# Feed forward of a hybrid decoder layer: right factors built in small steps, factor tiles regrouped, three units on unnormalised input, another order of plain and seven-product units

## The chip, the cores and the metric

One core of a Trainium2 chip. The metric is the device time of one execution in microseconds. Engines are named as the profile does: PE is TensorE's matrix product and PEld its weight load, DVE is VectorE, ACT is ScalarE, POOL is GpSimd, SP is SyncE, which issues nearly all DMAs.

## The reference, cut to what matters

One inference step of one decoder layer: 512 prompt tokens and 8 sample tokens (520 columns here), model width 1024. A mixer (retention, dilated attention, gates) is followed by a feed forward; the change touches the feed forward alone.

```python
h = h + mix
h = h + swiglu(rmsnorm(h, ln2_g), w_ffn_in, w_ffn_out)
y = rmsnorm(h, lnf_g)

def swiglu(xn, w_ffn_in, w_ffn_out):
    a, b = jnp.split(xn @ w_ffn_in, 2, axis=-1)     # hidden width 2816 = 22 x 128
    return (jax.nn.silu(a) * b) @ w_ffn_out
```

Everything is float32. To come near to that on TensorE, every operand of a product is split in two float32r parts: a high part (a copy, rounded) and a low part (operand minus high part). A product is then three: high x high, high x low, low x high.

## The kernel before, in words

**Layout.** Activations lie transposed: 128 rows of the model width per tile, 520 columns in two halves of 260 (HF). Weights stream from HBM as 194 pieces of 128 x 1024 (`raw`, four buffers, each loaded by SP when the low part of an earlier piece is done). Each piece falls into blocks of 128 x 512. For each block ScalarE makes the high part (`wh`, line 200) and VectorE the low part (`wl`, line 203), with six buffers of each; `advance` (lines 213 to 221) keeps them five blocks ahead of TensorE.

**The feed forward's order.** Hidden unit i (0 to 21) stands for 128 rows of a and 128 rows of b. `FFSEQ` (lines 28 to 32) lists the work: "in" 0 to 8, four "out" steps for the hidden rows 0 to 7, "in" 9 to 16, four "out" steps for rows 8 to 15, "in" 17 to 21. After the loop `LAST` and what follows it do the output for rows 16 to 21.

**Plain units.** `ffn_in(i)` calls `unit` twice, once for a and once for b: 8 steps of 6 products of 260 columns, 96 products per hidden unit, into a pair of PSUM banks. There are two such pairs, used in turn, so the evacuation of one half frees the bank pair that the half after the next writes. Silu(a) is made by ScalarE, the multiplication by b (`middle`) by VectorE.

**Seven-product units (quads).** The units in `INQ` and all eight "out" steps in the loop run through `quad` (line 285) instead, by Strassen's scheme in Winograd's form: seven products of half-size factors in the place of eight, 84 matrix products. `SEVEN` (line 283) lists for each of the seven products j the bank (0, 1 or 2) and the right factor x: bank 0 serves j = 0, 2, 4 and 6, bank 1 serves j = 1 and 5, bank 2 serves j = 3. Bank 0 (and 1) goes on accumulating after ScalarE has copied an intermediate state into a snapshot (`s`, line 312, after j = 0, 1, 2, 4). So the product j = 2 waits for the snapshot of j = 0, j = 4 for that of j = 2, j = 6 for that of j = 4. The next quad's first product writes what was bank 1, which the addition at line 1323 reads after j = 5; its second product writes what was bank 0, which the multiplication at line 1331 reads after j = 6. VectorE also makes the sums of weight blocks (lines 184, 188, 190).

**Right factors.** A quad needs, for each pair k of 128-row blocks, the four parts (two blocks, two halves) and four differences of them (one of the eight is unused on the output side), each as a high and a low part.
- For the input, `gen_factors` (line 1221) makes the normalised input, first the parts (lines 1227 to 1231), then the differences (lines 1242 to 1254), into `XH` and `XL`. It is a generator that advances by one step at each `pump`.
- For the output, `right` (line 315) works on `UF`, which holds the four parts of a pair of hidden units: four operations of 260 columns on VectorE, a copy of 1820 columns on ScalarE (line 321) and a subtraction of 1820 columns on VectorE (line 322). It is called after each odd unit up to 15, at one go; only the subtraction is deferred by three pumps.

**What sets the order.** Each engine works through its instructions in the order in which the program issues them. `pump` (line 123) is called between groups of products, 16 times in a plain unit and 14 times in a quad. It issues the operations that `later` has deferred and then advances the tracks named in `pattern` by one step each; P is the track in use in the feed forward. `finish` advances a track until a given generator is done.

**The unnormalised units.** The norm's factor `rs2` is known only after the last block of h. Units 0 and 1 (`NX = 2`, line 1265) therefore run on `X2`, the input without that factor, and multiply the result by `rs2` at evacuation (lines 1293 and 1302), one more VectorE operation for each half. From unit 2 the products read `XH` and `XL`. `UH`, the right factors' high parts, takes the place of `X2` after unit 1 (line 1364).

Of the kernel before, what the change touches and what calls it, by code (L numbers as in the profile page):

```python
# [18 lines left out]
HF, HT = 260, 256  # L19
# [18 lines left out]
def tile_hybrid_layer(  # L38
# [9 lines left out]
    V, A, G_, PE, SP = nc.vector, nc.scalar, nc.gpsimd, nc.tensor, nc.sync  # L48
# [3 lines left out]
    bpool = ctx.enter_context(tc.tile_pool(name="bpool", bufs=1))  # L52
# [9 lines left out]
    def halves(ap):  # L62
        return ap.rearrange("p (f c) -> p f c", f=2)
# [10 lines left out]
    def f32(ap):  # L74
        return ap.bitcast(F32)
# [24 lines left out]
    pattern = ["P"]  # L100
# [3 lines left out]
    def later(n, fn):  # L104
        delayed.append([n, fn])
# [176 lines left out]

    SEVEN = ((0, 0), (1, 3), (0, 4), (2, 1), (0, 5), (1, 2), (0, 6))

    def quad(xh, xl, snap, evac):

        s = pos[0] // 8
        pos[0] += 16
        nkp = QUADS[s]

        turn["busy"] ^= 1
        pms = {}
        for _ in range(2):
            i = turn["next"]
            pms[i] = bank_pair(i)[:, 0, :HF]
        out = [pms[turn["busy"]], pms[1 - turn["busy"]], None]
        begun = set()
        for j, (bank, x) in enumerate(SEVEN):
            advance(bid[s, 0] + j)
            if bank == 2:  # L300
                out[2] = abank("pc")[:, :HF]
            h, l = split[bid[s, 0] + j]
            for k in range(nkp):
                ks = slice(k * 128, k * 128 + 128)
                for w, r in ((h, xh), (h, xl), (l, xh)):
                    PE.matmul(out[bank], w[:, ks], r[:, k, x, :], start=bank not in begun, stop=k == nkp - 1 and r is xh and w is l,  # L306
                              skip_group_check=True)
                    begun.add(bank)
                if k % 2:
                    pump()  # L310
            if j in (0, 1, 2, 4):
                A.activation(snap[(0, 3, 1, None, 2)[j]], out[bank], AF.Copy)  # L312
            evac(j, out[bank])

    def right(t, hi, lo):

        V.tensor_tensor(t[:, 3, :], t[:, 0, :], t[:, 7, :], op=ALU.subtract)
        V.scalar_tensor_tensor(t[:, 4, :], t[:, 2, :], -1.0, t[:, 3, :], op0=ALU.mult, op1=ALU.subtract)
        V.tensor_tensor(t[:, 5, :], t[:, 2, :], t[:, 7, :], op=ALU.subtract)
        V.scalar_tensor_tensor(t[:, 6, :], t[:, 4, :], -1.0, t[:, 1, :], op0=ALU.mult, op1=ALU.subtract)  # L320
        A.activation(hi, t[:, 0:7, :], AF.Copy)
        later(3, lambda: V.tensor_tensor(lo, t[:, 0:7, :], f32(hi), op=ALU.subtract))
# [891 lines left out]


    pattern[:] = ["P"]
    XH = bpool.tile([128, 32, HF], F32R, tag="bg", name="XH")
    XL = fp.tile([128, 32, HF], F32R, name="XL")
    XH4, XL4 = (u.rearrange("p (k x) c -> p k x c", x=8) for u in (XH, XL))

    def gen_factors():
        yield from gen_norm2()
        xs = {}

        def one(c, out):
            x = ftmp("xn")
            V.scalar_tensor_tensor(x, hT[:, c, :], g2v[:, c:c + 1], rs2, op0=ALU.mult, op1=ALU.mult)
            xs[c] = x
            hi, lo = (u[:, c // 2, 1:3, :] if c % 2 else u[:, c // 2, 0::7, :] for u in (XH4, XL4))
            A.activation(hi, halves(x), AF.Copy)  # L1230
            later(2, lambda: V.tensor_tensor(lo, halves(x), f32(hi), op=ALU.subtract))

        for c in range(8):
            one(c, None)
            yield
            yield
        for k in range(4):
            x1, x2 = xs.get(2 * k), xs.get(2 * k + 1)
            if k < 3:
                x1, x2 = ftmp("xn"), ftmp("xn")  # L1240
                for c, x in ((2 * k, x1), (2 * k + 1, x2)):
                    V.scalar_tensor_tensor(x, hT[:, c, :], g2v[:, c:c + 1], rs2, op0=ALU.mult, op1=ALU.mult)
# [44 lines left out]
    def ffn_in(i):  # L1287
        s = {}

        def ev_fa(pm, s=s):  # L1290
            t = ftmp("fa")
            if i < NX:
                V.tensor_tensor(halves(t), pm, halves(rs2), op=ALU.mult)
                A.activation(t, t, AF.Silu)
            else:
                A.activation(halves(t), pm, AF.Silu)  # L1296
            s["a"] = t

        def ev_fb(pm, i=i, s=s):
            if i < NX:  # L1300
                t = ftmp("fb")
                V.tensor_tensor(halves(t), pm, halves(rs2), op=ALU.mult)
                pm = halves(t)
            middle(i, lambda out: V.tensor_tensor(out, pm, halves(s["a"]), op=ALU.mult))

        src = (lambda k: (X2[:, k, :], X2[:, 8 + k, :])) if i < NX else xnsrc
        pa = unit(8, src, ev_fa if i else None)
        pb = unit(8, src, ev_fb if i else None)
        if i == 0:
            while not normed:  # L1310
                run_delayed()
                step("P")
            ev_fa(pa)
            ev_fb(pb)

    def ffn_in_quad(i):
        s12, s35 = snaps()
        t = ftmp("fa")

        def evac(j, bank):  # L1320
            if j in (3, 5):
                f = (j - 3) // 2
                V.tensor_tensor(t[:, f * HF:(f + 1) * HF], bank, s12[:, f, :], op=ALU.add)
                if f:
                    A.activation(t, t, AF.Silu)
            elif j == 4:
                later(1, lambda: V.tensor_tensor(s35[:, 0, :], s35[:, 0, :], s35[:, 1, :], op=ALU.add))
            elif j == 6:
                def mult(out):
                    for f, x in ((1, s35[:, 0, :]), (0, bank)):  # L1330
                        V.scalar_tensor_tensor(out[:, f, :], x, -1.0, t[:, f * HF:(f + 1) * HF], op0=ALU.mult, op1=ALU.mult)  # L1331
# [254 lines left out]
```

## Time and profile before

| | |
|---|---|
| median of 3 runs | 1333.28 us (1331.69 to 1336.47) |
| profiled execution | 1334.04 us, its span 1332.2 us |
| mean granted TensorE clock | 0.989 |
| PE busy | 1285.9 us (97%) |
| DVE busy | 818.0 us (61%) |
| ACT busy | 570.6 us (43%) |
| feed forward "in" units 0 to 4 | about 928 to 1003.9 us |
| from unit 5 to unit 21 with the eight "out" steps | 1003.9 to 1280.6 us |

How to read the rows. A row of a group names line, engine, operation, output and inputs, shapes and count, then busy time, mean nanoseconds of one, idle time of the engine before them and what ended it. A row of an engine's timeline has start, duration, engine, line, operation and, in brackets, the idle time before it and its releaser. A row of the chain of waits has start, duration, engine, output and line; "x36" counts instructions. A row of the windows has the stretch, its length, the busy time of PE, PEld, DVE, ACT and POOL with counts, the granted clock, the DMA share and GB/s. TensorE's products are pipelined: 260 columns start every 0.12 us though each is shown with 0.28.

### The profile page before, as it was taken

To read this page: it belongs to the slowest core of one execution; us is meant where nothing else is said; L and a number is where in the kernel's file an instruction comes from. 1 tells how busy PE (TensorE), PEld (TensorE's weight loads), DVE (VectorE), ACT (ScalarE), POOL (GpSimd) and SP (SyncE) were. 2 spreads that over 40 slices of the span, in tenths; PEclk is the share of its full clock that TensorE was granted. 3 is DMA by queue.
4 is the path that set the end of the run, shared out by engine and by line. 5 is a ranking of instruction groups with operands and counts; after the bars stand their busy time and mean duration, and the time that the engine had idled before them with its cause. 6 is when DMAs were issued, how large, how long until landed. Compare 5 with 4: busy or idle time off the path is not lost.

```text
span 1332.2 us, 25611 instructions
## 1 busy us (share of the span) xinstructions
PE 1285.9 (97%) x10465; PEld 1251.6 (94%) x10465; DVE 818.0 (61%) x1713; ACT 570.6 (43%) x1080; POOL 83.3 (6%) x69
## 2 busy tenths in 40 slices
PE   8999999999999999999999999999879999999997
PEld 7999999998988999999999999999879899999997
DVE  7867636747655523244545455486777787679765
ACT  4564334535453522243444433333344455445542
POOL 3601001010002000000000000030000000000000
PEclk9999999999999999999999999999989999999999
DMA  6266236646484232454645556433223232233321
GB/s 219 81 229 229 90 117 206 225 143 230 145 301 157 84 99 89 135 148 127 185 135 171 161 159 205 160 118 122 63 64 96 74 114 84 80 98 112 101 87 65
DMA packets 89783, 183.35 MB, mean 138 GB/s; under 512 B 12025, under 2 KB 33945, under 8 KB 89665
## 3 DMA queue, kind: packets, MB, share of 16 engines
q1 hardware_dynamic: 88944, 180.64, 43.0%
q8 instruction: 82, 1.34, 0.4%
q10 hardware_dynamic: 720, 1.07, 0.2%
q14 instruction: 37, 0.30, 0.1%
HBM read 155.70 MB, written 25.98 MB: 136 GB/s over the span
## 4 chain that ended last, share of the span: by engine, by line
PE 84%; DVE 7%; DMA 3%; issue 3%; ACT 2%; POOL 1%; SPq 1%; DVEq 0%; ACTq 0%
PE pm L250 58%; PE pm L306 11%; PE sp L331 3%; PE pc L306 2%; DMA vb<-vd 2%; PE sp L560 2%; PE sp L578 2%; DVE wl L203 1%; PE pm L1474 1%; PE sp L970 1%; PE sp L512 1%; ACT wh L200 1%; PE sp L920 1%; PE oacc L673 1%; PE sacc L1115 1%
## 5 line engine op out<-in xcount | busy, mean ns | idle before, releaser
L250 PE MATMUL pm<-X,wh 128*128 128x260 f32 x3328 | 550.7, 287 | 4.7 <-DVE X L363 3.6
L250 PEld LDWEIGHTS pm<-X,wh 128*128 128x128 f32 x3328 | 460.5, 189 | 19.4 <-issue 8.3
L203 DVE TENSOR_TENSOR wl<-raw,wh 128x512 fp32r<-128x512 f32 x384 | 275.0, 720 | 165.6 <-ACT wh L200 162.0
L250 PE MATMUL pm<-X,wl 128*128 128x260 f32 x1664 | 336.2, 284 | 0.0
L200 ACT ACTIVATE wh<-raw 128x512 fp32r<-128x512 f32 x384 | 238.7, 625 | 210.1 <-PE pm L250 159.1
L250 PEld LDWEIGHTS pm<-X,wl 128*128 128x128 f32 x1664 | 257.8, 189 | 0.4 <-DVE wl L373 0.4
L306 PE MATMUL pm<-XH,wh 128*128 128x260 f32 x288 | 83.2, 289 | 11.6 <-ACT s L312 9.4
L250 PE MATMUL pm<-GA,wh 128*128 128x260 f32 x512 | 82.2, 283 | 0.0
L306 PE MATMUL pm<-XL,wh 128*128 128x260 f32 x288 | 81.8, 284 | 0.0
L306 PE MATMUL pm<-XH,wl 128*128 128x260 f32 x288 | 81.6, 283 | 0.0
L250 PEld LDWEIGHTS pm<-GA,wh 128*128 128x128 f32 x512 | 70.1, 188 | 0.0
L306 PEld LDWEIGHTS pm<-XH,wh 128*128 128x128 f32 x288 | 54.5, 189 | 14.1 <-ACT s L312 10.6
L250 PE MATMUL pm<-XH,wh 128*128 128x260 f32 x256 | 53.2, 290 | 9.9 <-ACT fa L1296 5.4
L628 ACT ACTIVATE kv<-vb,ks 128x512 f32<-128x512 f32 x64 | 44.2, 714 | 29.6 <-DMA vb<-vd 29.0
L340 POOL TENSOR_TENSOR r<-v,cst 128x4 f32<-128x4 f32 (+4 forms) x14 | 17.6, 1261 | 609.1 <-DVE v L338 609.1
L306 PE MATMUL pm<-UH,wh 128*128 128x260 f32 x192 | 54.4, 283 | 0.9 <-DVE UF L1331 0.9
L306 PEld LDWEIGHTS pm<-XL,wh 128*128 128x128 f32 x288 | 54.7, 190 | 0.0
L306 PEld LDWEIGHTS pm<-XH,wl 128*128 128x128 f32 x288 | 54.6, 190 | 0.0
L306 PE MATMUL pm<-UL,wh 128*128 128x260 f32 x192 | 54.2, 282 | 0.0
L203 DVE TENSOR_TENSOR wl<-qq,wh 128x512 fp32r<-128x512 f32 x60 | 41.2, 687 | 21.1 <-ACT wh L200 20.8
L306 PE MATMUL pm<-UH,wl 128*128 128x260 f32 x192 | 54.1, 282 | 0.0
L663 DVE SCALAR_TENSOR_TENSOR st<-st,kv 128x512 f32<-128x512 f32 x64 | 45.3, 712 | 12.5 <-ACT kv L628 12.5
(324 smaller groups left out, 2185.7 us busy)
## 6 DMA issues: line engine op xcount, KB each, us to landing
raw<-wall SPq DMA_DIRECT2D x192, 512.0 KB
st<-state SPq DMA_DIRECT2D x64, 256.0 KB
out<-st SPq DMA_DIRECT2D x64, 256.0 KB
area<-ck SPq DMA_DIRECT2D x24, 512.0 KB
vb<-vd SPq DMA_DIRECT2D x32, 256.0 KB
area<-qd SPq DMA_DIRECT2D x12, 512.0 KB
cb<-cd SPq DMA_DIRECT2D x4, 768.0 KB
xr<-xT SPq DMA_DIRECT2D x8, 260.0 KB
```

Source lines behind the costliest of these rows:

```text
L200: A.activation(h, r, AF.Copy)
L203: V.tensor_tensor(l, r, f32(h), op=ALU.subtract)
L250: PE.matmul(pm[:, f, :HF], w, x[f] if isinstance(x, tuple) else x[:, f * HF:(f + 1) * HF], start=first, stop=last)
L306: PE.matmul(out[bank], w[:, ks], r[:, k, x, :], start=bank not in begun, stop=k == nkp - 1 and r is xh and w is l, skip_group_check=True)
L331: PE.transpose(out, in_, ident[:n, :n])
L340: G_.tensor_tensor(r[:rows, :ncol], v[:rows, :ncol], mhalf[:rows].to_broadcast([rows, ncol]), op=ALU.pow)
L512: PE.matmul(sp[:, :T - i0], x[:, dt, jb * 128:(jb + 1) * 128], y[:, dt, i0:], start=i == 0, stop=i == len(mm) - 1)
L560: PE.matmul(sp[:, i0:], v[x][:, jb, c * 128:(c + 1) * 128], scs[y][:, SCO[jb]:SCO[jb] + T - i0], start=jb == 0 and x == y, stop=jb == 3 an ...
L578: PE.matmul(sp, kt[x][:, jb, dt * 128:(dt + 1) * 128], v[y][:, jb, :], start=jb == 0 and x == y, stop=jb == 3 and x == 1)
L628: A.activation(kvs[i][:, :DV], vbs[b], AF.Copy, scale=ks[:, dt, b:b + 1])
L663: V.scalar_tensor_tensor(sts[i], sts[i], GAMMA[h], kvs.pop(i)[:, :DV], op0=ALU.mult, op1=ALU.add)
L673: PE.matmul(acc[32 * j:32 * j + 32, :], om[:, bb, :], ys[bb], start=b == 3, stop=b == NS - 1, tile_position=(0, 32 * j), skip_group_check= ...
```

## The change

- `INQ` names other units: plain are now 0 to 5, 8, 12, 16 and 20 (before: 0 to 4, 7, 10, 13, 16 and 19). Both lists have 12 quads.
- `NX` is 3: unit 2 also runs on the unnormalised input.
- `right` becomes a generator on track S with 12 steps; its copy and its subtraction are cut into pieces of 780, 520 and 520 columns. It is pushed after the odd units from 3 on; for the pair (0, 1) it is pushed in the evacuation of unit 2 and finished there at once, ahead of unit 2's own multiplication, which overwrites `UF`. Each even unit and each first "out" step finishes what is left.
- The pattern is "PS" instead of "P".
- The input's factors lie in `XP` (high and low of the parts) and `XT` (high and low of the differences) instead of `XH` (high of all eight) and `XL` (low of all). The differences are split in two halves of 520 columns each, with one step between copy and subtraction.
- In a quad's last evacuation the multiplication that reads the bank comes before the one that reads the snapshot.
- `UH` is opened in the evacuation of unit 2, ahead of `right`.

```diff
-INQ = (5, 6, 8, 9, 11, 12, 14, 15, 17, 18, 20, 21)
+INQ = (6, 7, 9, 10, 11, 13, 14, 15, 17, 18, 19, 21)
...
-    def quad(xh, xl, snap, evac):
+    def quad(factor, snap, evac):
...
-                for w, r in ((h, xh), (h, xl), (l, xh)):
-                    PE.matmul(out[bank], w[:, ks], r[:, k, x, :], start=bank not in begun, stop=k == nkp - 1 and r is xh and w is l,
+                for w, i in ((h, 0), (h, 1), (l, 0)):
+                    PE.matmul(out[bank], w[:, ks], factor(i, k, x), start=bank not in begun, stop=k == nkp - 1 and w is l,
                               skip_group_check=True)
...
-    XH = bpool.tile([128, 32, HF], F32R, tag="bg", name="XH")
-    XL = fp.tile([128, 32, HF], F32R, name="XL")
+    XP = bpool.tile([128, 2, 4, 4, HF], F32R, tag="bg", name="XP")
+    XT = fp.tile([128, 2, 4, 4, HF], F32R, name="XT")
...
-            hi, lo = XH4[:, k, 3:7, :], XL4[:, k, 3:7, :]
-            A.activation(hi, t, AF.Copy)
-            yield
-            yield
-            V.tensor_tensor(lo, t, f32(hi), op=ALU.subtract)
-            yield
+            for j in (0, 2):
+                hi, lo = XT[:, 0, k, j:j + 2, :], XT[:, 1, k, j:j + 2, :]
+                A.activation(hi, t[:, j:j + 2, :], AF.Copy)
+                yield
+                V.tensor_tensor(lo, t[:, j:j + 2, :], f32(hi), op=ALU.subtract)
+                yield
...
+    pattern[:] = ["PS"]
     push("P", gen_factors())
...
-    NX = 2
+    NX = 3
...
+        if i == NX - 1:
+            rights.append(push("S", right(UF, 0)))
+        if i % 2 == 0 and rights:
+            finish("S", rights[-1])
         mult(UF[:, 1:3, :] if i % 2 else UF[:, 0::7, :])
         if i % 2 and i > 1:
-            k = i % 8 // 2
-            right(UF, UH4[:, k], UL4[:, k])
+            rights.append(push("S", right(UF, i % 8 // 2)))
...
+    def right(t, k):
+
+        yield
+        V.tensor_tensor(t[:, 3, :], t[:, 0, :], t[:, 7, :], op=ALU.subtract)
+        V.scalar_tensor_tensor(t[:, 4, :], t[:, 2, :], -1.0, t[:, 3, :], op0=ALU.mult, op1=ALU.subtract)
+        yield
+        V.tensor_tensor(t[:, 5, :], t[:, 2, :], t[:, 7, :], op=ALU.subtract)
+        V.scalar_tensor_tensor(t[:, 6, :], t[:, 4, :], -1.0, t[:, 1, :], op0=ALU.mult, op1=ALU.subtract)
+        yield
+        for j, n in ((0, 3), (3, 2), (5, 2)):
+            hi, lo = (u[:, k, j:j + n, :] for u in (UH4, UL4))
+            A.activation(hi, t[:, j:j + n, :], AF.Copy)
+            yield
+            yield
+            V.tensor_tensor(lo, t[:, j:j + n, :], f32(hi), op=ALU.subtract)
+            yield
...
+            if i == NX - 1:
+                open_u()
             middle(i, lambda out: V.tensor_tensor(out, pm, halves(s["a"]), op=ALU.mult))
...
-                    for f, x in ((1, s35[:, 0, :]), (0, bank)):
+                    for f, x in ((0, bank), (1, s35[:, 0, :])):
                         V.scalar_tensor_tensor(out[:, f, :], x, -1.0, t[:, f * HF:(f + 1) * HF], op0=ALU.mult, op1=ALU.mult)
...
         if kind == "out":
+            if i == 0:
+                finish("S", rights[-1])
             ffn_out(i)
             continue
...
-        if i == NX - 1:
-            UH = bpool.tile([128, 28, HF], F32R, tag="bx", name="UH")
-            UH4, UL4 = (u.rearrange("p (k x) c -> p k x c", x=7) for u in (UH, UL))
-            UHp, ULp = (u.rearrange("p (k f) c -> p k (f c)", f=2) for u in (UH, UL))
-            right(UF, UH4[:, 0], UL4[:, 0])
```

More of the change, by code (lines that the diff above doesn't have):

```diff
@@ L313, in quad @@
             evac(j, out[bank])
[L315 to L322, printed above, removed]
     def sbank(name="sp"):
@@ L1216, in tile_hybrid_layer @@
     pattern[:] = ["P"]
-    XH = bpool.tile([128, 32, HF], F32R, tag="bg", name="XH")
-    XL = fp.tile([128, 32, HF], F32R, name="XL")
-    XH4, XL4 = (u.rearrange("p (k x) c -> p k x c", x=8) for u in (XH, XL))
+    XP = bpool.tile([128, 2, 4, 4, HF], F32R, tag="bg", name="XP")
+    XT = fp.tile([128, 2, 4, 4, HF], F32R, name="XT")
     def gen_factors():
@@ L1228, in one @@
             xs[c] = x
-            hi, lo = (u[:, c // 2, 1:3, :] if c % 2 else u[:, c // 2, 0::7, :] for u in (XH4, XL4))
+            hi, lo = (XP[:, i, c // 2, 1:3, :] if c % 2 else XP[:, i, c // 2, 0::3, :] for i in range(2))
             A.activation(hi, halves(x), AF.Copy)
@@ L1249, in gen_factors, with xfactor, ufactor @@
             yield
-            hi, lo = XH4[:, k, 3:7, :], XL4[:, k, 3:7, :]
-            A.activation(hi, t, AF.Copy)
-            yield
-            yield
-            V.tensor_tensor(lo, t, f32(hi), op=ALU.subtract)
-            yield
-    def xnsrc(k):
-        return tuple((u[:, k // 2, k % 2, :], u[:, k // 2, 2 if k % 2 else 7, :]) for u in (XH4, XL4))
+            for j in (0, 2):
[4 more added lines that the diff above has]
+                yield
+    def xnsrc(k):
+        return tuple((XP[:, i, k // 2, k % 2, :], XP[:, i, k // 2, 2 if k % 2 else 3, :]) for i in range(2))
+    def xfactor(i, k, x):
+        return XP[:, i, k, x, :] if x < 3 else XT[:, i, k, x - 3, :]
+    def ufactor(i, k, x):
+        return (UL4 if i else UH4)[:, k, x, :]
+    pattern[:] = ["PS"]
     push("P", gen_factors())
@@ L1281, in middle, with open_u @@
             return
+        if i == NX - 1:
+            rights.append(push("S", right(UF, 0)))
+        if i % 2 == 0 and rights:
+            finish("S", rights[-1])
         mult(UF[:, 1:3, :] if i % 2 else UF[:, 0::7, :])
         if i % 2 and i > 1:
-            k = i % 8 // 2
-            right(UF, UH4[:, k], UL4[:, k])
+            rights.append(push("S", right(UF, i % 8 // 2)))
+    rights = []
+    def right(t, k):
[13 more added lines that the diff above has]
+            yield
+    def open_u():
+        nonlocal UH4, UL4, UHp, ULp
+        UH = bpool.tile([128, 28, HF], F32R, tag="bx", name="UH")
+        UH4, UL4 = (u.rearrange("p (k x) c -> p k x c", x=7) for u in (UH, UL))
+        UHp, ULp = (u.rearrange("p (k f) c -> p k (f c)", f=2) for u in (UH, UL))
+    UH4 = UL4 = UHp = ULp = None
     def ffn_in(i):
@@ L1329, in mult @@
                 def mult(out):
-                    for f, x in ((1, s35[:, 0, :]), (0, bank)):
+                    for f, x in ((0, bank), (1, s35[:, 0, :])):
                         V.scalar_tensor_tensor(out[:, f, :], x, -1.0, t[:, f * HF:(f + 1) * HF], op0=ALU.mult, op1=ALU.mult)
                 middle(i, mult)
-        quad(XH4, XL4, [s12[:, 0, :], s12[:, 1, :], s35[:, 0, :], s35[:, 1, :]], evac)
+        quad(xfactor, [s12[:, 0, :], s12[:, 1, :], s35[:, 0, :], s35[:, 1, :]], evac)
     def ffn_out(c):
@@ L1352, in evac @@
                 V.tensor_tensor(h2[:, 0, :], h2[:, 0, :], bank, op=ALU.subtract)
-        quad(UH4, UL4, [s12[:, 0, :], s12[:, 1, :], s35[:, 0, :], s35[:, 1, :]], evac)
+        quad(ufactor, [s12[:, 0, :], s12[:, 1, :], s35[:, 0, :], s35[:, 1, :]], evac)
     for kind, i, seven in FFSEQ:
         if kind == "out":
+            if i == 0:
+                finish("S", rights[-1])
             ffn_out(i)
```

## The prediction

> **What bounds the kernel now.** I read the page first, then the feed forward's stretch in the windows, the chain of waits and the timelines of single engines.
>
> ```profile
> span 1332.2 us, 25611 instructions
> PE 1285.9 (97%) x10465; PEld 1251.6 (94%) x10465; DVE 818.0 (61%) x1713; ACT 570.6 (43%) x1080; POOL 83.3 (6%) x69
> 955.00:987.00 32.00, 21.86 (x147) 20.82 (x147) 26.31 (x46) 11.12 (x15) 0.00 (x0) 0.84 0.17 50
> ```
>
> TensorE is the bound: 46 us of 1332.2 are idle. The last row (span, PE, PEld, DVE, ACT, POOL, clock) is the hole: VectorE is busier than TensorE there, and the granted clock is 0.84. The other place is the feed forward's main stretch:
>
> ```profile
> 1003.85 4.31 PE pm L306 x36
> 1019.72 1.71 PE pm L306 x12
> 1027.20 11.50 PE pm L250 x96
> 1038.72 0.70 DVE UF L1304
> 1079.01 8.62 PE pm L306 x72
> 1087.62 1.45 PE pc L306 x12
> 1130.79 2.60 PE pm L306 x12
> 1248.29 11.48 PE pm L250 x96
> 1280.56 7.93 PE pm L250 x66
> ```
>
> A quad without stalls takes 8.62 + 1.45 = 10.07 us, a plain unit 11.48. From unit 5's start (1003.85) to LAST (1280.56) pass 276.7 us for 20 quads and 5 plain units, which need 201.4 + 57.4 = 258.8. So **17.9 us are lost** there. The change keeps all these numbers: 12 quads in "in", 8 in "out", 10 plain units. TensorE's floor does not move; only losses can.
>
> TensorE's own timeline says where (in brackets: idle before, and who ended it):
>
> ```profile
> 964.26 0.80 PE L250 MATMUL pm<-XH,wh 128*128 128x260 f32 x2 [2.69 <-DVE fb L1302]
> 977.06 0.80 PE L250 MATMUL pm<-XH,wh 128*128 128x260 f32 x2 [5.38 <-ACT fa L1296]
> 986.36 0.51 PE L250 MATMUL pm<-XH,wh 128*128 128x260 f32 x2 [1.52 <-DVE UF L1304]
> 1015.70 0.39 PE L306 MATMUL pm<-XH,wh 128*128 128x260 f32 x1 [0.32 <-DVE UF L1331]
> 1019.72 0.39 PE L306 MATMUL pm<-XH,wh 128*128 128x260 f32 x1 [2.33 <-ACT s L312]
> 1043.50 0.39 PE L306 MATMUL pm<-XH,wh 128*128 128x260 f32 x1 [1.95 <-ACT s L312]
> 1049.93 0.39 PE L306 MATMUL pm<-XH,wh 128*128 128x260 f32 x1 [0.41 <-ACT s L312]
> 1054.28 0.39 PE L306 MATMUL pm<-UH,wh 128*128 128x260 f32 x1 [0.89 <-DVE UF L1331]
> 1130.79 0.39 PE L306 MATMUL pm<-XH,wh 128*128 128x260 f32 x1 [2.33 <-ACT s L312]
> ```
>
> The stalls sit in quads during which `right` runs: 6, 8, 12 and 14, each following an odd quad or unit. Where `right` falls into a plain unit (10, 16), nothing stalls. The queues in quad 6:
>
> ```profile
> 1013.62 0.62 ACT L200 ACTIVATE wh<-qq 128x512 fp32r<-128x512 f32 x1
> 1014.27 0.69 DVE L203 TENSOR_TENSOR wl<-qq,wh 128x512 fp32r<-128x512 f32 x1 [0.63 <-ACT wh L200]
> 1014.88 0.42 DVE L1331 SCALAR_TENSOR_TENSOR UF<-s,fa 128x260 f32<-128x260 f32 x1
> 1015.22 0.42 DVE L1331 SCALAR_TENSOR_TENSOR UF<-pm,fa 128x260 f32<-128x260 f32 x1
> 1015.56 0.42 DVE L317 TENSOR_TENSOR UF<-UF 128x260 f32<-128x260 f32 x1
> 1017.15 1.72 ACT L321 ACTIVATE UH<-UF 128x1820 fp32r<-128x1820 f32 x1 [2.92 <-DVE UF L320]
> 1018.78 0.61 ACT L200 ACTIVATE wh<-qq 128x512 fp32r<-128x512 f32 x1
> 1019.30 0.37 ACT L312 ACTIVATE s<-pm 128x260 f32<-128x260 f32 x1
> 1020.04 2.05 DVE L322 TENSOR_TENSOR UL<-UF,UH 128x1820 fp32r<-128x1820 f32 x1
> ```
>
> Both queues run in order. `right`'s copy waits 2.92 us for its four differences with the snapshot behind it, then takes 1.72; product 2 needs that snapshot (bank 0) and starts at 1019.72. Unstalled, by 1013.92 (1003.85 + 10.07) + 2 x 1.44, it would have started at 1016.8.
>
> **The change, part by part.** Starts lie 0.61 apart for a low part (1014.27, 1014.88) and 0.34 for 260 columns (1014.88, 1015.22): 0.08 less than durations. Longer and shorter work, and a product's modelled time:
>
> ```profile
> L306 PE MATMUL pm<-XL,wh 128*128 128x260 f32 x288 | 81.8, 284 | 0.0
> L322 DVE TENSOR_TENSOR UL<-UF,UH 128x1820 fp32r<-128x1820 f32 x8 | 16.4, 2048 | 0.0
> L1273 DVE TENSOR_TENSOR UL<-fu,UH 128x520 fp32r<-128x520 f32 x5 | 3.5, 701 | 2.9 <-ACT UH L1272 2.8
> L184 DVE TENSOR_TENSOR qq<-raw,raw 128x1024 f32<-128x1024 f32 x20 | 24.4, 1219 | 0.3 <-DMA raw<-wall 0.3
> L1272 ACT ACTIVATE UH<-fu 128x520 fp32r<-128x520 f32 x5 | 3.2, 639 | 8.9 <-DVE fu L1331 5.7 <-DVE fu L1304 3.2
> ```
>
> *Swapped product order.* The bank is read first, so it is free 0.34 us earlier: the 0.32 at 1015.70 and its like go. No cost: both multiplications follow at once.
>
> *Pieces of `right`.* From 520 to 1820 columns VectorE takes 1.04 ns a column, so 780 columns take 0.97. In the queue (0.08 less each) the three low parts take 0.89 + 0.62 + 0.62 = 2.13 instead of 1.97; with four differences, 3.5 us. A quad's own VectorE work: seven low parts 4.3, sums 1.14 + 0.61 + 0.61, five short ones 1.7, together 8.3 of 10.07. So a quad with `right` has 11.8: VectorE must fall behind by about 1.8, whatever the order. [...]
>
> *Where `right` falls now.* After units 3, 7, 11, 15 it runs during plain 4, 8, 12, 16 (room: two low parts per 5.7 us). It stays in quads 6, 10, 14. Its 12 steps end within 14 pumps, so `finish` finds nothing left, and also nothing before the first "out".
>
> Quad 10, from the start T of its first product, on unit 6's rows as a model (there T = 1013.92 and the second multiplication leaves the queue at 1015.56, T + 1.65). VectorE ends, in queue order: low part 2.25, two differences 2.95, two more 3.65, low part 4.25, sum 5.4, low part 6.0, first piece 6.9, sum 7.5, low part 8.1, an addition 8.4, second piece 9.05, low part 9.65. ScalarE's third copy and the snapshot before product 6 stand behind a weight copy that needs the sum of 7.5; the snapshot ends at 9.15 where 8.6 was wanted: 0.5 lost. VectorE has the snapshots' sum, a low part and the third piece until 11.3, and only then the addition that frees the next quad's first bank, at 11.75, where 9.15 + 1.44 = 10.6 was wanted: 1.1 lost. Then follow Silu (0.64) and what the rows show from the weight copy at 1013.62 to the multiplication at 1014.88 (1.26); the multiplication frees the second bank at 14.0, wanted at 11.75 + 1.44 = 13.2: 0.8 lost. Together 2.4. Quad 14 likewise. Quad 6 follows a plain unit; there (7, which ends at 1027.20 + 11.50) the multiplication is through 0.7 after the end instead of 1.65, so I take 2.4 - 0.8 = 1.6. For what is left after 17 and 18 I add 0.1. Loss after: 1.6 + 2.4 + 2.4 + 0.1 = 6.5. Bounds: 2 (the waits inside VectorE's queue, as the 0.63 at 1014.27, take up the arrears) and 12: every one as bad as 8 before, 1.95 + 0.41 + 0.89 idle and 0.16 each, by which a product's modelled 0.28 outlasts the 0.12 to the next, 3.7, and 0.9 more. I take 6.5: **gain 11.4**.
>
> *Third unnormalised unit.* VectorE's queue in the hole:
>
> ```profile
> 963.51 0.69 DVE L1302 TENSOR_TENSOR fb<-pm,rs 128x520 f32<-128x520 f32 x1
> 964.24 0.70 DVE L1304 TENSOR_TENSOR UF<-fb,fa 128x520 f32<-128x520 f32 x1
> 968.79 0.69 DVE L203 TENSOR_TENSOR wl<-raw,wh 128x512 fp32r<-128x512 f32 x1 [2.37 <-ACT wh L200]
> 972.51 1.43 DVE L1242 SCALAR_TENSOR_TENSOR xn<-hT,vec,rs 128x520 f32<-128x520 f32 x2
> 985.61 0.69 DVE L1304 TENSOR_TENSOR UF<-pm,fa 128x520 f32<-128x520 f32 x1
> ```
>
> Up to 964.24 + 0.61 = 964.85 VectorE does the same in the same order, so unit 2's second half still starts at 964.26: no gain, and the clock falls as before. Then `right` is absent (before: four differences, 2.37 idle, 1.97). After, in order: low part, two pieces of 520, xn twice 1.35, low part, four differences 1.4, wait, piece: 971.3. The new multiplication by rs2 frees unit 3's first bank at 972.0, so unit 3 starts at 972.1 instead of 977.06. Its second half waits for the second new multiplication, behind two low parts, xn, differences and three pieces: 979.75 (before 986.36), idle 1.8. Then comes the burst of `finish`: four differences, three copies, three low parts, multiplication, until 984.6, and k = 3's factors behind it; unit 3's Silu stands on ScalarE behind their copies and ends at 988.3, where unit 4 wanted 985.6: idle 2.6. Two halves of 5.74 end unit 4 at 999.8; before 1003.85. For a lower clock after 2.6 idle I add 1.1 (below). **Gain 3.0**, bounds -2 (both gaps stretched) and 8 (the burst hides).
>
> The clock: after 2.33 idle, 12 products took 2.60 us at 1130.79 but 1.71 at 1019.72, 1.45 being undisturbed; after 2.69 and 5.38 the first two took 0.80 instead of 0.40. A fall costs 1 to 2 us, I take 1.8 at 6 in 10. [...]
>
> *Two tiles XP and XT; hi and lo together.* Same bytes, and the timeline shows unit 2 waiting factor by factor, never for the differences: nothing. XT's halves add 4 x 0.08, counted above.
>
> **Sum.** 11.4 + 3.0 = 14.4. The profiled execution took 1334.04 (span 1332.2 and 1.84 around it), giving 1319.6; the median of the three runs lies 0.76 below it: **1319**.
>
> **The rivals.** (a) The steps hide wholly: quads lose 2, the burst hides behind the products already banked, entry gains 8: 15.9 + 8 = 24 gained, 1309. For it: around 1079 quads follow one another without a gap. Against: 11.8 us of work in 10.07. (b) The waits only move: `right`'s pieces stand ahead of the snapshots as the lump did; three quads at 3.7 and the entry at 0: 17.9 - 11.1 = 6.8, 1326.5. For it: 0.41 and 0.89 were lost before to VectorE's arrears alone. This is also the case in which the change does not do what it says. (c) Slower: VectorE never catches up in the runs of seven and three quads. If the idle that its waits on ScalarE leave (0.63 in each quad's rows) is not absorbed, each `right` in a quad costs all of its 3.5 us and 1.9 of copies (the 1.72 at 1017.15, and two more starts at 0.1) and lowers the clock (1.8), 3 x 7.2 = 21.6, and the burst puts its 5 us in the open: 17.9 - 21.6 - 5 = -8.7, 1342. It decides when product 0 of quads 11 and 15 waits over 4 us. Against: plain units follow within two quads.
>
> **How the numbers follow.** Forecast (1313 to 1324) 0.58; (a) 0.16; (b) 0.21, of which 0.07 comes out within 0.3% (4 us, about what a measurement of this kernel can tell from no change); (c) 0.05. So faster 0.88, same 0.07, slower 0.05. The range 1309 to 1328 reaches (a)'s and (b)'s times and leaves out their far ends.
>
> **What would show it.** Right: no 2.33 gaps for `s` in quads; in 10 and 14 a gap of 0.3 to 0.6 for `s` at product 6 and about 1 for `fa`, then for `UF` in 11 and 15; unit 3 starting near 972, unit 4 near 988. Wrong: unit 2's second half starting elsewhere than 964.3, gaps over 2 us after quad 10, or stalls in 7 and 18.

## The result and the profile after

| | before | after |
|---|---|---|
| median | 1332.67 us (4 runs, 1331.69 to 1336.47) | 1318.73 us (4 runs, 1318.19 to 1319.36) |
| ratio | | 0.989, 95% interval 0.987 to 0.9911 |
| profiled execution's span | 1332.2 us | 1317.1 us |
| mean granted TensorE clock | 0.989 | 0.993 |

14 us faster; the forecast was 1319 in 1309 to 1328. The page after, its head:

```profile
span 1317.1 us, 25670 instructions
PE 1282.0 (97%) x10465; PEld 1247.7 (95%) x10465; DVE 820.3 (62%) x1735; ACT 574.9 (44%) x1100; POOL 83.2 (6%) x69
```

TensorE's 10465 products are the same, VectorE and ScalarE have slightly more to do (22 and 20 instructions, 2.3 and 4.3 us busy). What went is mostly TensorE's waiting: its idle time falls from 46.3 to 35.1 us; the other 3.9 us are busy time, at a mean granted clock of 0.993 instead of 0.989. Its timeline after, rows with idle time before them:

```profile
942.46 0.71 PE L250 MATMUL pm<-X,wh 128*128 128x260 f32 x4 [0.54 <-DVE fa L1320]
963.79 1.21 PE L250 MATMUL pm<-X,wh 128*128 128x260 f32 x4 [3.79 <-ACT XT L1242]
978.96 0.72 PE L250 MATMUL pm<-XP,wh 128*128 128x260 f32 x4 [1.88 <-DVE fb L1329]
986.23 0.74 PE L250 MATMUL pm<-XP,wh 128*128 128x260 f32 x4 [1.30 <-ACT fa L1323]
1020.21 0.51 PE L306 MATMUL pm<-XP,wh 128*128 128x260 f32 x2 [0.65 <-DVE fa L1352]
1022.47 0.51 PE L306 MATMUL pm<-XT,wh 128*128 128x260 f32 x2 [0.55 <-DVE UF L1360]
1102.52 0.50 PE L306 MATMUL pm<-XT,wh 128*128 128x260 f32 x2 [0.37 <-ACT s L312]
1104.96 0.51 PE L306 MATMUL pm<-XP,wh 128*128 128x260 f32 x2 [0.75 <-DVE fa L1352]
1107.22 0.50 PE L306 MATMUL pm<-XT,wh 128*128 128x260 f32 x2 [0.55 <-DVE UF L1360]
...
```

Before, 5.38 stood ahead of unit 3 and 2.33 or 1.95 for a snapshot in each of four quads; both kinds are gone. In their place stand small gaps at the right-laden quads, those during which `right` runs: three each at 10 and 11 and, the like, at 14 and 15 (1147 to 1152), for the snapshot `s` at product 6, then the bank that the addition into `fa` frees, then the one that the multiplication into `UF` frees; at 6 and 7 only the last two. The chain of waits gives the boundaries:

```profile
1009.47 4.33 PE pm L306 x36
1225.68 1.71 PE pm L306 x12
1265.45 7.91 PE pm L250 x66
```

**A common measure.** All kernels below have the same work from the start of unit 1 (942.46 here) to LAST (1265.45 here): 20 quads and 9 plain units. At the prediction's 10.07 and 11.48 us these need 304.7. What is above it is loss, in each kernel's own profile, and free of what the earlier stages do, which differed by up to 4 us among executions. "Entry" is the part up to the first quad, less the plain units in it; "quads" is the rest.

| kernel | unit 1 to LAST | loss | entry | quads | median, ratio (95%) |
|---|---|---|---|---|---|
| before | 337.6 | 32.9 | 14.9 | 17.9 | |
| after | 323.0 | 18.3 | 9.6 | 8.6 | 1318.73, 0.989 (0.987 to 0.9911) |
| two units unnormalised | 322.9 | 18.2 | 9.5 | 8.7 | 1320.71, 0.99 (0.9879 to 0.9921) |
| old list | 319.9 | 15.2 | 9.6 | 5.6 | 1315.87, 0.9863 (0.9845 to 0.9881) |
| right at one go | 333.3 | 28.6 | 13.1 | 15.4 | 1327.72, 0.9962 (0.9944 to 0.998) |
| old order of multiplications | 324.0 | 19.3 | 9.6 | 9.6 | 1317.83, 0.9882 (0.9865 to 0.99) |
| low parts on GpSimd | 329.9 | 25.2 | 12.1 | 13.1 | 1323.28, 0.9935 (0.9917 to 0.9954) |
| steps only | 322.7 | 18.0 | 11.0 | 7.0 | 1317.19, 0.9883 (0.9865 to 0.99) |
| old list, late copy | 319.1 | 14.4 | 9.6 | 4.8 | 1315.47, 0.9871 (0.9857 to 0.9886) |
| the same with GpSimd | 327.4 | 22.7 | 12.2 | 10.5 | 1321.75, 0.9917 (0.9898 to 0.9935) |
| extra low part | 327.5 | 22.8 | 11.8 | 10.9 | 1324.3, 0.9919 (0.9889 to 0.9949) |
| late differences | 321.7 | 17.0 | 8.3 | 8.7 | 1315.67, 0.9857 (0.9831 to 0.9884) |
| list and split right | 316.6 | 11.9 | 9.6 | 2.3 | 1310.55, 0.9823 (0.979 to 0.9855) |
| all together | 308.8 | 4.1 | 1.5 | 2.7 | 1304.91, 0.978 (0.9759 to 0.9801) |

Where two losses differ by only a few us, the intervals of the ratios overlap; there I go by the loss, which is from one profiled execution of each kernel. Where the same code recurs it repeats within 0.1 us (the entry is 9.6 in five of these kernels), unless the granted clock falls at another gap: two units unnormalised and steps only issue the same work up to unit 4, and their entries lost 9.5 and 11.0.

### The profile page after: what moved, and what is told of

Read it like the earlier page. It is cut to its first block, busy times and chain, and to the rows that moved or that the text cites. A ratio compares the mean times of both kernels' runs of the same rounds, so it can differ in the third digit from the quotient of the medians.

```text
span 1317.1 us, 25670 instructions
## 1 busy us (share of the span) xinstructions
PE 1282.0 (97%) x10465; PEld 1247.7 (95%) x10465; DVE 820.3 (62%) x1735; ACT 574.9 (44%) x1100; POOL 83.2 (6%) x69
## 3 DMA queue, kind: packets, MB, share of 16 engines
q1 hardware_dynamic: 88944, 180.64, 43.7%
## 4 chain that ended last, share of the span: by engine, by line
PE 85%; DVE 7%; DMA 2%; issue 2%; ACT 2%; POOL 1%; SPq 0%; DVEq 0%; ACTq 0%
PE pm L250 59%; PE pm L306 12%; PE sp L322 3%; PE pc L306 2%; DMA vb<-vd 2%; PE sp L551 2%; PE sp L569 2%; PE pm L1500 1%; DVE wl L203 1%; PE sp L961 1%; PE sp L503 1%; PE sp L911 1%; ACT wh L200 1%; PE oacc L664 1%; PE sacc L1106 1%
## 5 line engine op out<-in xcount | busy, mean ns | idle before, releaser
L250 PE MATMUL pm<-X,wh 128*128 128x260 f32 x3392 | 561.8, 288 | 8.1 <-ACT XT L1242 3.8
L250 PEld LDWEIGHTS pm<-X,wh 128*128 128x128 f32 x3392 | 470.2, 190 | 23.1 <-issue 8.3
L250 PE MATMUL pm<-XP,wh 128*128 128x260 f32 x448 | 72.2, 283 | 3.2 <-DVE fb L1329 1.9
L306 PE MATMUL pm<-XT,wh 128*128 128x260 f32 x384 | 71.9, 286 | 2.6 <-DVE UF L1360 1.7
L250 PEld LDWEIGHTS pm<-XP,wh 128*128 128x128 f32 x448 | 61.3, 188 | 3.6 <-issue 2.1
L306 PEld LDWEIGHTS pm<-XT,wh 128*128 128x128 f32 x384 | 59.1, 188 | 4.8 <-DVE UF L1360 2.7
L306 PE MATMUL pm<-XT,wl 128*128 128x260 f32 x192 | 54.2, 282 | 0.0
L654 DVE SCALAR_TENSOR_TENSOR st<-st,kv 128x512 f32<-128x512 f32 x64 | 45.4, 713 | 11.4 <-ACT kv L619 11.4
L250 PE MATMUL pm<-GA,wl 128*128 128x260 f32 x256 | 51.6, 283 | 0.0
L312 ACT ACTIVATE s<-pm 128x260 f32<-128x260 f32 x80 | 30.8, 386 | 45.6 <-PE pm L306 45.3
L200 ACT ACTIVATE wh<-qq 128x512 fp32r<-128x512 f32 x60 | 37.3, 629 | 30.4 <-PE pm L250 17.4
```

What stands on the lines that cost most here:

```text
L200: A.activation(h, r, AF.Copy)
L250: PE.matmul(pm[:, f, :HF], w, x[f] if isinstance(x, tuple) else x[:, f * HF:(f + 1) * HF], start=first, stop=last)
L306: PE.matmul(out[bank], w[:, ks], factor(i, k, x), start=bank not in begun, stop=k == nkp - 1 and w is l, skip_group_check=True)
L654: V.scalar_tensor_tensor(sts[i], sts[i], GAMMA[h], kvs.pop(i)[:, :DV], op0=ALU.mult, op1=ALU.add)
```

## The experiments

**Two units unnormalised** is the changed kernel with one number set back.

```diff
-    NX = 3
+    NX = 2
```

> The changed kernel with NX = 2, all else as changed. Theory A (the lump of right was what filled the hole; the third unnormalised unit only moves VectorE's work about): unit 3 starts within 1 us of the changed kernel's, its second half about 980.7 instead of 978.96, unit 4 again near 986, the time 1318 to 1320. Theory B (the prediction's own term: the third unit is what frees unit 3's bank): unit 3 starts near 977 as before, 5 us are lost, 1323 to 1325.

Loss 18.2 against 18.3, and 1320.71 us: nearer Theory A, though 0.7 over its range. Unit 3 starts 1.1 us later counted from unit 1, but unit 4 no later (43.7 us after unit 1 against 43.8), although unit 2's products now read the normalised factors. The waits over 0.3 us are others: 2.69 ahead of unit 2's second half and then, ahead of unit 3's,

```profile
981.14 0.74 PE L250 MATMUL pm<-XP,wh 128*128 128x260 f32 x4 [2.16 <-DVE UF L1333]
```

instead of 3.79, 1.88 and 1.30. The one number changes two things: with two units, `right` for the pair (0, 1) is pushed a unit earlier and runs in steps during unit 2, not at once in unit 2's evacuation. So the run shows that the third unnormalised unit together with that burst brought nothing in this execution; what each does alone is not shown. Below, steps only has the same entry and lost 1.5 more there, so the third unit may save that much where the clock falls.

**Old list** sets back the choice of plain units.

```diff
-INQ = (6, 7, 9, 10, 11, 13, 14, 15, 17, 18, 19, 21)
+INQ = (5, 6, 8, 9, 11, 12, 14, 15, 17, 18, 20, 21)
```

> The changed kernel with the old list of quads (5, 6, 8, 9, 11, 12, 14, 15, 17, 18, 20, 21). Theory A (what counts is in how many quads right runs, three or four, and that VectorE has 11.8 us of work in a quad of 10.07): quads 6, 8, 12, 14 lose about 1.7 each instead of three losing 1.8, 2.7 and 2.8, and one pair after unit 17 less loses 0.6; sum 7.5 against 8.6, the time 1317 to 1319. Theory B (one plain unit in four is what spares the quads): four quads with right at 2.7, 1320 to 1323.

It is faster, by more than Theory A had: quads lose 5.6 instead of 8.6. Gaps over 0.1 us are left after 8 and 14 only. Right-laden quads 6 and 12, which a plain unit follows, lose 0.3 each: in the chain of waits quad 5 begins at 998.38 and plain unit 7 at 1018.79, 20.41 for two quads of 10.07.

```profile
998.38 4.33 PE pm L306 x36
...
1018.79 11.55 PE pm L250 x96
```

So my count of quads with `right` was the wrong count. What matters is how many of them are followed by another quad: two in the old list, three in the new. "One plain unit in four" made this change 3 us worse by the loss than it could have been.

**Right at one go** puts the lump back into the changed kernel.

```diff
-        for j, n in ((0, 3), (3, 2), (5, 2)):
-            hi, lo = (u[:, k, j:j + n, :] for u in (UH4, UL4))
-            A.activation(hi, t[:, j:j + n, :], AF.Copy)
...
+        A.activation(hi, t[:, 0:7, :], AF.Copy)
+        low = lambda: V.tensor_tensor(lo, t[:, 0:7, :], f32(hi), op=ALU.subtract)
+        low() if now else later(3, low)
```

> The changed kernel with right at one go again (one copy and one low part of 1820 columns; low part deferred by three pumps, at once for the pair (0, 1)); list, third unit, order of the two multiplications as changed. Theory A (the copy of 1820 columns ahead of the snapshot is what costs): quads 6, 10 and 14 lose 4.4 to 5 each as 8 and 14 did before, 7.3 becomes about 14, the time 1325 to 1327. Rival (VectorE's arrears cost the same however right is cut): 1318 to 1320.

9 us slower than the changed kernel by the medians, 10.3 by the loss: 6.8 in the quads (Theory A had 7) and 3.5 in the entry, where the lump of the pair (0, 1) now holds unit 4. The gaps for `s` are back, and the clock falls behind them: after 1.93 idle it was 0.81 from 1016 to 1018 and 0.50 from 1018 to 1020, after 2.66 it was 0.50 from 1103 to 1105. On this list the steps are worth 10.3 of the 14.6 us of loss that the whole change took away.

```profile
986.46 1.20 PE L250 MATMUL pm<-XP,wh 128*128 128x260 f32 x4 [3.22 <-ACT fa L1315]
1016.06 0.51 PE L306 MATMUL pm<-XT,wh 128*128 128x260 f32 x2 [1.93 <-ACT s L312]
1103.07 0.80 PE L306 MATMUL pm<-XT,wh 128*128 128x260 f32 x2 [2.66 <-ACT s L312]
```

**Old order of multiplications** reads the snapshot first and the bank second.

```diff
-                    for f, x in ((0, bank), (1, s35[:, 0, :])):
+                    for f, x in ((1, s35[:, 0, :]), (0, bank)):
```

> The changed kernel with the old order of the two multiplications in a quad's last evacuation (snapshot first, bank second). Theory A: the bank comes free 0.34 us later, which shows at product 1 after 6, 9, 10, 13 and 14, so 5 x 0.34 = 1.7 us more; after 17 and 18 nothing changes, because there the copy of the product stands ahead of the snapshot on ScalarE and needs both multiplications: 1320 to 1321. Rival (other work hides it): within 0.5 us of the changed kernel.

Neither theory: 1.0 us more by the loss, three places of 0.34 and not five, which the medians (0.9 less) cannot tell from nothing. After 6, 10 and 14 the gap for `UF` is 0.89 instead of 0.55, as expected. After 9 and 13 a gap of 0.33 is back, but the later gap of 0.37 at product 6 of the same quad is not there any more: the order only moved that wait. After 17 and 18 it moves too, as expected: with the old order the gap is at product 1,

```profile
1223.92 0.51 PE L306 MATMUL pm<-XT,wh 128*128 128x260 f32 x2 [0.33 <-DVE fu L1360]
```

with the new one at product 2, where ScalarE's copy of `fu` needs both multiplications and stands ahead of the weight copy and the snapshot (changed kernel, ScalarE's timeline; TensorE resumes at 1225.68):

```profile
1224.19 0.64 ACT L1269 ACTIVATE UH<-fu 128x520 fp32r<-128x520 f32 x1 [1.44 <-DVE fu L1360]
1224.74 0.62 ACT L200 ACTIVATE wh<-qq 128x512 fp32r<-128x512 f32 x1
1225.26 0.37 ACT L312 ACTIVATE s<-pm 128x260 f32<-128x260 f32 x1
```

**Low parts on GpSimd** was to take 2.1 us per pair off VectorE.

```diff
-            V.tensor_tensor(lo, t[:, j:j + n, :], f32(hi), op=ALU.subtract)
+            G_.tensor_tensor(lo, t[:, j:j + n, :], f32(hi), op=ALU.subtract)
```

> The changed kernel with right's three low parts on GpSimd instead of VectorE; nothing is left out. Theory A (VectorE's arrears are what stalls the quads with right: 11.8 us of work in 10.07): 2.1 us leave VectorE's queue, 9.7 are left, and the losses of 1.8, 2.7 and 2.8 us in and after quads 6, 10 and 14 fall under 0.5 each; some 6 us less than the changed kernel, 1312 to 1313. Rival (ScalarE's copies ahead of the snapshots are what stalls): the 0.37 at product 6 stays and most of the rest, 1317 to 1319. Third: GpSimd is so slow at 780 columns that the next multiplication into UF waits for it: 1320 or more.

None of the three: 4.6 us slower than the changed kernel, a time in the third's range but not for its reason, since no multiplication waited for GpSimd to finish. VectorE's own instructions were held. Its timeline and GpSimd's at quad 10:

```profile
1097.87 0.42 DVE L1295 TENSOR_TENSOR UF<-UF 128x260 f32<-128x260 f32 x1
1098.21 2.10 DVE L1296 SCALAR_TENSOR_TENSOR UF<-UF 128x260 f32<-128x260 f32 x1
...
1103.78 0.42 DVE L1352 TENSOR_TENSOR fa<-pc,s 128x260 f32<-128x260 f32 x1
1104.13 1.43 DVE L203 TENSOR_TENSOR wl<-raw,wh 128x512 fp32r<-128x512 f32 x1
1105.48 1.53 DVE L1356 TENSOR_TENSOR s<-s 128x260 f32<-128x260 f32 x1
```

```profile
1098.04 1.99 POOL L1303 TENSOR_TENSOR UL<-UF,UH 128x780 fp32r<-128x780 f32 x1 [55.47 <-PE pm L306]
1103.66 3.07 POOL L1303 TENSOR_TENSOR UL<-UF,UH 128x520 fp32r<-128x520 f32 x2 [3.63 <-PE pm L306]
```

The operation that takes 0.42 us elsewhere takes 2.10 while GpSimd's 1.99 run, and ends 0.28 after it. So VectorE was held longer than the low parts would have kept it busy. As a test of the theory it worked from the other side: with VectorE later, the gaps for `fa` after the three quads grew from between 0.65 and 0.75 to between 1.35 and 1.42, and those for `s` at product 6 of 10 and 14 from 0.37 to 1.20 and 1.19.

**The same with GpSimd** joined this to the old list and the late copy below.

> The changed kernel with the old list, the deferred copy in whole and right's low parts on GpSimd. Theory A: on top of the deferred copy the two losses of 1.8 us after quads 8 and 14 go, 315 to 316 us from unit 1's start to LAST, the time 1311 to 1312.5, below both kernels. Rival (no gain from GpSimd, since it only waits for the same copies): 1314 to 1315.

Neither: 8.3 us more loss than without GpSimd. VectorE is held in the same way: at 1035.76 a sum of weight blocks that takes 1.22 us elsewhere took 2.88, beside 1.93 us of GpSimd.

**Steps only** keeps of the change the small steps and the regrouped tiles; list, `NX` and order are the old ones (the three diffs above together).

> The changed kernel with the old list, NX = 2 and the old order of the two multiplications: of the change only right's small steps, the track and the regrouped tiles are left. Theory A (the steps are the whole of the gain): from unit 1's start to LAST 320 to 321 us, where the kernel before has 337.6 and the changed one 323.0; the time 1315 to 1318. Rival (the parts work only together): 1322 or more.

The loss is 18.0, 14.9 less than before: the steps, with the tiles that this run keeps, make the whole gain. That it is 2 us over the expected 320 to 321 shows in the entry: after a gap of 2.17 three halves, 144 products, took 19.05 us, where 17.2 is normal, as the clock had fallen (0.62 from 980 to 984); the quads lose 1.4 more than with the new order.

```profile
978.55 0.75 PE L250 MATMUL pm<-XP,wh 128*128 128x260 f32 x4 [2.17 <-DVE UF L1333]
```

**Old list, late copy** defers the copy in `whole`.

```diff
-        A.activation(hi, t, AF.Copy)
-        later(2, lambda: V.tensor_tensor(lo, t, f32(hi), op=ALU.subtract))
+        later(3, lambda: A.activation(hi, t, AF.Copy))
+        later(5, lambda: V.tensor_tensor(lo, t, f32(hi), op=ALU.subtract))
```

> The changed kernel with the old list, and in whole the copy deferred by three pumps, behind the next quad's first snapshot, the low part by five. Theory A (after units 17 and 20 the copy stands ahead of that snapshot on ScalarE and holds the quad's product 2): 0.5 to 0.6 us less for each of the two pairs than with the old list alone, which had 319.9 us from unit 1's start to LAST: now 318.7 to 319. Rival (VectorE is what is late there): no difference.

0.8 less loss than the old list. The two pairs 17, 18 and 20, 21 lose 0.3 each instead of 0.6, which is Theory A; the medians, 0.4 apart, cannot tell it.

**Extra low part** issues the last low part of each `right` twice.

```diff
             V.tensor_tensor(lo, t[:, j:j + n, :], f32(hi), op=ALU.subtract)
+            if j == 5:
+                V.tensor_tensor(lo, t[:, j:j + n, :], f32(hi), op=ALU.subtract)
```

> The changed kernel with right's last low part (520 columns, VectorE, 0.61 us in the queue) issued twice, nothing else. Theory A (VectorE's arrears in quads with right): product 0 of quads 7, 11 and 15 waits 0.6 longer, 3 x 0.6 = 1.8 us more from unit 1's start to LAST (324.8 against 323.0); plain units with right show nothing. Rival (the stalls come from ScalarE's copies ahead of the snapshots): no change.

The quads lose 2.2 to 2.3 more; the gaps for `fa` after 6, 10 and 14 are 1.37, 1.46 and 1.46 instead of 0.65, 0.75 and 0.75, while those for `s` and `UF` stay. 0.61 us of VectorE's work in the queue came out of TensorE's time as 0.7, three times: the extra piece stands right ahead of the addition, and the next quad waits for that (the third piece, the extra one, the addition; then TensorE, quad 11).

```profile
1108.78 0.69 DVE L1303 TENSOR_TENSOR UL<-UF,UH 128x520 fp32r<-128x520 f32 x1
1109.51 0.70 DVE L1305 TENSOR_TENSOR UL<-UF,UH 128x520 fp32r<-128x520 f32 x1
1110.12 0.42 DVE L1354 TENSOR_TENSOR fa<-pm,s 128x260 f32<-128x260 f32 x1
```

```profile
1110.60 0.51 PE L306 MATMUL pm<-XP,wh 128*128 128x260 f32 x2 [1.46 <-DVE fa L1354]
```

That shows VectorE's arrears, work that it is behind with, as the cause of the gap for `fa`. It cannot show the cause of the one for `s`, which comes earlier in the queue. The rest, 2.2, is in the entry, where the extra piece lengthened the burst after unit 2 and the clock fell once more (0.70 from 988.8 to 991, after 2.02 idle).

**Late differences** puts idle steps ahead of the input's differences.

```diff
+        for _ in range(8):
+            yield
         for k in range(4):
             x1, x2 = xs.get(2 * k), xs.get(2 * k + 1)
```

> The changed kernel with eight idle steps between the input's parts and its differences, so that unit 1's second evacuation (the multiplication by rs2 that frees unit 2's second bank) no longer stands behind k = 0's xn and differences, 2.7 us, in VectorE's queue. Theory A (VectorE's order at that place holds unit 2): unit 2's second half starts 2.5 to 2.8 us earlier, the clock does not fall there (another 1.3), 9.6 us lost in the entry become 4 to 6; 319 us or less from unit 1's start to LAST, the time 1313 to 1316. Rival (VectorE's sum of work up to unit 4 is the bound, the waits only move to units 3 and 4): within 1 us of the changed kernel.

Half of each theory: the median lies in Theory A's range, the 321.7 us do not. Unit 2's second half starts 18.5 us after unit 1 instead of 21.3, and after 0.99 idle instead of 3.79. But only 1.3 is kept: the copies of the differences of k = 2 now stand ahead of unit 3's Silu on ScalarE and wait 3.86 us for VectorE, and unit 4 waits 3.32 and runs on a lower clock (0.50 from 982 to 984).

```profile
959.38 0.71 PE L250 MATMUL pm<-X,wh 128*128 128x260 f32 x4 [0.99 <-DVE fb L1331]
972.70 0.72 PE L250 MATMUL pm<-XP,wh 128*128 128x260 f32 x4 [1.64 <-DVE fb L1331]
982.00 1.24 PE L250 MATMUL pm<-XP,wh 128*128 128x260 f32 x4 [3.32 <-ACT fa L1325]
```

```profile
980.14 1.31 ACT L1244 ACTIVATE XT<-ts 128x520 fp32r<-128x520 f32 x2 [3.86 <-DVE ts L1238]
981.36 0.59 ACT L1325 ACTIVATE fa<-pm 128x520 f32<-128x520 f32 x1
```

**List and split right** follows from the old list's result: plain units where they follow or hold `right`, and for the three cases left (after 5, 11 and 13) two of the three pieces one unit later. It also defers the copy in `whole`, by the edit of old list, late copy, which is not printed again here.

```diff
-INQ = (6, 7, 9, 10, 11, 13, 14, 15, 17, 18, 19, 21)
+INQ = (5, 6, 9, 11, 12, 14, 15, 17, 18, 19, 20, 21)
...
-        if i % 2 == 0 and rights:
+        if rights and i not in (6, 12, 14):
             finish("S", rights[-1])
...
-            rights.append(push("S", right(UF, i % 8 // 2)))
+            rights.append(push("S", right(UF, i % 8 // 2, 8 if i in (5, 11, 13) else 0)))
...
         for j, n in ((0, 3), (3, 2), (5, 2)):
+            for _ in range(wait if j == 3 else 0):
+                yield
```

> The changed kernel with another list (plain: 0 to 4, 7, 8, 10, 13, 16, so that each right but the one after 13 runs in a plain unit or in a quad before a plain unit), the deferred copy in whole, and after 5, 11 and 13 only the first piece of right in the next unit, the other two one unit later. Theory A (arrears are paid only at the next quad's banks, and two quads can share them): of the losses of the old list with the deferred copy (5.6 less 1.2) the two of 1.8 us go and none comes in their place: 315 to 316 us from unit 1's start to LAST, the time 1311 to 1313. Rival (the gain of the old list lay in something else): 1315 or more.

Theory A, 0.6 us over its 315 to 316 and with a time 0.5 under its range: quads lose 2.3 in all. From the first quad to LAST one gap is left, 0.23, at product 1 of quad 15; the rest are losses of 0.3 at single boundaries that show no gap.

**All together** builds on list and split right, keeps its deferred copy and its split, makes the plain units 0 to 5, 8, 10, 13 and 16, and spreads the differences.

```diff
-INQ = (6, 7, 9, 10, 11, 13, 14, 15, 17, 18, 19, 21)
+INQ = (6, 7, 9, 11, 12, 14, 15, 17, 18, 19, 20, 21)
...
         for k in range(4):
+            for _ in range((8, 12, 3, 9)[k]):
+                yield
             x1, x2 = xs.get(2 * k), xs.get(2 * k + 1)
```

> Built on the list with the split right and the deferred copy: plain now 0 to 5, 8, 10, 13, 16, and idle steps before the differences of each k (8, 12, 3 and 9), so that they spread over units 2 to 5 and none stands ahead of unit 3's Silu. Theory A (the entry's losses are VectorE's and ScalarE's order at single places, and VectorE's sum of work has room once it may run into unit 5): of the 9.6 us lost between unit 1 and the first quad 6 go, of the split about 0.6 are lost more at quads 6 and 7; about 311 us from unit 1's start to LAST, the time 1303 to 1307. Rival (VectorE's sum of work is the bound, as unit 4 gave back half with the late differences): 1309 to 1311, no better than the list with the split right.

Theory A: loss 4.1, 1304.91 us, 0.978 of the kernel before (0.9759 to 0.9801). After unit 1's first product TensorE has these three gaps up to LAST:

```profile
961.58 0.71 PE L250 MATMUL pm<-X,wh 128*128 128x260 f32 x4 [0.96 <-DVE fb L1333]
1013.79 0.51 PE L306 MATMUL pm<-XT,wh 128*128 128x260 f32 x2 [0.23 <-DVE UF L1364]
1139.74 0.51 PE L306 MATMUL pm<-XT,wh 128*128 128x260 f32 x2 [0.23 <-DVE UF L1364]
```

VectorE's sum of work was not the bound of the entry: as in the changed kernel units 0 to 5 are plain and no work is left out, yet the entry loses 1.5 instead of 9.6. Its order was.

## Why the prediction was right, and where its steps were not

The sum was right, 14.4 forecast against 15.1 in the spans, with two terms off in opposite directions: the quads gained 9.3 instead of 11.4, the entry 5.3 instead of 3.0; 0.55 came from before unit 1, where nothing was changed. That the sum came so near is luck in part: errors of 2.1 and 2.3 cancelled.

*Quads, right-laden.* The mechanism held step by step. For quad 10 the waits were forecast at 0.5 (snapshot), 1.1 (`fa`) and 0.8 (`UF`). Against an undisturbed 1.44 us from product to product, the three products start 0.54, 1.00 and 0.82 later; the idle times of 0.37, 0.75 and 0.55 show less, since every gap hides 0.16 or more. From the "out" steps' start at 1042.89 to plain unit 12 at 1116.11, 73.22 us for seven quads, 2.7 are lost (forecast 2.4); 14 and 15 lose 2.8 (2.4), 6 and 7 lose 1.8 (1.6). That VectorE's arrears cause the wait for `fa` is shown by the extra low part. For `s` only low parts on GpSimd speaks for it, where VectorE was held and the gap grew with it. The wait for `UF` stayed at 0.55 in both runs: it follows from the chain that the prediction gave, from the addition by Silu and the weight copy to the multiplication.

*Quads after 17 and 18.* This was the mis-sized term: 0.1 forecast, 1.3 measured (71.77 us from 1172.09 to 1243.86, for seven quads). The step "the 0.32 at 1015.70 and its like go" failed for these: the deferred copy shows that ScalarE's copy of `fu` was the next in line. Stalls in 7 and 18 were also named as signs of being wrong, and both came. For 7 (0.65 and 0.55) that sign contradicts the prediction's own sum, which has the banks freed by quad 6 late at the next quad; for 18 it marks this term.

*Entry.* "Unit 2's second half still starts at 964.26: no gain" was right: 21.33 us after unit 1's start, before 21.25. Unit 3's second half was forecast 36.7 us after it and came after 36.5. Unit 4 was forecast after 45.3 and came after 43.8, and its 1.1 us for a lower clock, an estimate, did not occur; its wait was 1.30 and not 2.6, and the granted clock after it 1.00 (986 to 988). The failed step is the burst of `finish`, taken at 5 us with copies behind the differences: the first piece holds three of the four parts and no difference, and ScalarE made its copy before VectorE's first difference (rows of the two timelines; the burst lasted 3.6, from 978.73 to 982.32).

```profile
976.97 0.84 ACT L1300 ACTIVATE UH<-UF 128x780 fp32r<-128x780 f32 x1
979.65 1.32 ACT L1300 ACTIVATE UH<-UF 128x520 fp32r<-128x520 f32 x2 [1.85 <-DVE UF L1293]
```

```profile
978.73 0.42 DVE L1292 TENSOR_TENSOR UF<-UF 128x260 f32<-128x260 f32 x1
980.22 2.18 DVE L1303 TENSOR_TENSOR UL<-UF,UH 128x780 fp32r<-128x780 f32 x3
982.32 0.70 DVE L1333 TENSOR_TENSOR UF<-fb,fa 128x520 f32<-128x520 f32 x1
```

*What the sum hid.* I booked the entry's gain under the third unnormalised unit; without it the entry loses 9.5 or 11.0 (the two executions above) against 9.6, so the steps alone gain 5.4 or 3.9 there, where the whole change gains 5.3. With the lump in place it may have been worth 1.8 (13.1 in right at one go, 14.9 before). And I booked the gain of the quads under pieces and list together; the list alone costs 3. Rival (b), "the waits only move", was right for the order of the two multiplications at four places, and wrong for `right`. Rival (c) had its mechanism, VectorE behind, but plain units take the arrears up, and product 0 of 11 and 15 waited 0.75 where (c) had over 4.

That the two regrouped tiles are worth nothing was not tried by itself; steps only kept them.

## What to carry to other kernels

When two engines work in order through queues that TensorE waits on, look for the long instruction that itself waits and stands ahead of a short one that TensorE needs; each cut cost 0.07 us of VectorE's time here (2.10 us from the first of three low parts to the next instruction, 1.96 for the one of 1820 columns), and the steps were worth more than all the rest. Work that put VectorE behind cost 0.3 us where a plain unit followed (6 and 12 in the old list) and 1.8 to 2.8 where a quad did (6, 10 and 14 in the changed kernel): it is paid where the next consumer of that engine is close, so place it where the following stage leaves room, or let two stages share it. Two terms that are right in the sum can be wrong in their causes, and one run with each part undone tells, if undoing it moves nothing else.

## What the runs showed of the hardware that was not expected

VectorE's instructions were held while GpSimd worked: 2.10 us for an operation of 0.42, ending 0.28 after GpSimd's 1.99 on 780 columns, and 1.43 and 1.53 for two others, 0.69 and 0.43 elsewhere, during two of 520 columns that took 3.07 together (rows above). All three read two operands from SBUF. The addition into `fa` at 1103.78, which reads one of its operands from PSUM, took its usual 0.42 beside GpSimd, and so did two more like it in this run, at 1017.64 and 1149.79 (0.34 to VectorE's next start, as usual). The holds were 1.68 of GpSimd's 1.99 us, and 0.74 and 1.10 of its 3.07; why, no run shows.

The granted clock fell in some executions after gaps that did not lower it in others: after 2.17 idle in steps only (0.62 from 980 to 984), but not after 2.16 at the same place of the same work in two units unnormalised (1.00 from 983 to 987); after 1.93 in right at one go (0.50 from 1018 to 1020), but not after 1.88 in the changed kernel (0.72 for the next four products, 0.71 after a gap of 0.54). After 3.79 the next four took 1.21 (0.50 from 964 to 966). So the length of a gap near 2 us did not tell here whether the clock falls after it; what does stays open.
